# Order edges for the input and attention stages of a hybrid decoder block

## The chip, the cores and the metric

The kernel runs on one core of a Trainium2 chip. The metric is the device time of one launch in microseconds (us); three runs of the kernel before gave 2033.87, 2034.86 and 2029.52 us, median 2033.87. This kernel's runs of one program differ by up to 0.26%, so a difference within 0.3% (6 us) counts as no change here.

The core has five engines that each work through a queue of instructions in a fixed order: PE (matrix multiplication, with PEld for its weight loads), DVE (vector), ACT (scalar and evictions), POOL, and SP, which in this kernel issues nearly all DMAs. An instruction that waits for a semaphore holds up everything behind it on its own engine.

## The reference

One decoder layer on 1024 tokens plus 16 learned ones, model width 1024, in float32:

```python
xn = rms_norm(h, g_pre_mix)
b_c, c_c, h_c, q, k, v, g_conv, g_attn = split(xn @ w_in)      # 8 blocks of 1024
y_conv = b_c * causal_dwconv(c_c * h_c, conv_w_mix)
o = stick_breaking_attention(q, k, v)                          # 16 heads of 64
merged = sigmoid(g_conv + b0) * (y_conv @ w_proj_conv) \
       + sigmoid(g_attn + b1) * (o @ w_proj_attn)
h = h + rms_norm(merged @ w_out, g_post_mix)
u, g = split(rms_norm(h, g_pre_ffn) @ w_up_gate)               # 2 x 2816
h = h + rms_norm((gelu(causal_dwconv(u, conv_w_ffn)) * g) @ w_down, g_post_ffn)

# stick breaking, for z = q k / 8 and s < t:
A[t, s] = sigmoid(z_ts) * prod over s < j < t of (1 - sigmoid(z_tj));  o = A @ v
```

## The kernel before, in words

Every matrix product is made of three float32r matmuls on values split into a high and a low part: `hi` is a rounded copy (ACT, a CAST) and `lo` is what the rounding left (a subtraction on DVE or POOL). A weight block of 128x1024 is loaded by SP into a tile `raw`, becomes `whi` (line 457, ACT) and `wlo` (line 369, two halves on DVE or POOL), and then serves 24 steps of three matmuls each (lines 345 to 347).

The program has these stages in the trace: the input norm (to about 52 us); the input products with `w_in`, as plain blocks and as pairs by Strassen's method (52 to 558); attention (558 to 1014), in whose gaps PE computes 13 further blocks of gate columns of `w_in`; then the branch projections, `w_out`, the up projection and the down projection.

Attention goes by 8 pairs of heads, 2 heads per pair, and 3 groups of 3 query blocks (114 queries each) per head. For each head SP loads six tiles `qh`, `kk`, `ql` from DRAM (`load_h`, lines 934 to 941), and for each pair `vv` (`load_v`, lines 923 to 926). For a query block:

- PE makes the scores `z` (lines 965 and 966), ACT the sigmoids `fl` (line 971), and DVE one running product along the keys over `fl` in place (line 982, a TENSOR_TENSOR_SCAN of up to 1040 elements).
- Per block of keys, PE transposes the scanned `fl` into a PSUM tile `tp` (line 1001), ACT copies it to `ah` (line 1006), DVE subtracts to get `al` (line 447, the *lowering*), and PE multiplies `ah` and `al` with `vv` into `av` (lines 1016 and 1017).
- ACT and DVE or POOL add the finished `av` into `ot` (lines 1039 to 1046), which SP stores once per pair.

What sets the order: the input stage and the attention stage are each planned by the class `Plan`. It holds tasks with an engine, an estimated cost, a key and buffer slots, plays them through its own clock, and emits the instructions in the order in which that clock started them. The instructions then go to the framework's scheduler. It takes them with the emitted order as priority, but plays them through a cost model of its own, and where an instruction isn't ready by that model it may place a later one of the same engine ahead of it. What it arrives at is the fixed order of each engine's queue. The function `in_program_order` can forbid that for a range of instructions: it ties each instruction to the one before it on the same engine, by an edge that gives an order and no semaphore.

```python
def in_program_order(tc, nc, first, last):
    before = {}
    for ins in list(nc.cur_bb.bb.instructions)[first:last]:
        if ins.engine in before:
            tc.add_manual_dep(ins, before[ins.engine].name, ...)
        before[ins.engine] = ins
```

It is called once, in the last line of `block_kernel`, with `first` (the number of instructions when the input stage's plan begins, line 440) and `last` (the number when the attention stage's plan has run, line 1075). Much later, in the loop over the groups of the down projection, stands `last = gi == len(groups) - 1`. After that loop `last` is `True`, which in a slice is 1, so that in the kernel before the range is empty and no instruction is tied.

Of the kernel before, what the change touches and what calls it, by code (L numbers as in the profile page):

```python
# [135 lines left out]
def block_kernel(ctx, tc, x, meta_tokens, g_pre_mix, w_in, channels, w_proj_conv,  # L136
                 w_proj_attn, w_out, g_post_mix, g_pre_ffn, w_up_gate, w_down,
                 g_post_ffn, out):
    nc = tc.nc
# [297 lines left out]
    tmp_e = sring.tile([P, 512], F32, name="tmp_e")  # L437
    snap_t = sring.tile([P, 2, 3, HS], F32, name="snap_e")

    first = len(nc.cur_bb.bb.instructions)  # L440
    plan = Plan({"raw": 2, "whi": 0, "wlo": 0, "ap": 4, "wk": 5, "st": 8, "xw": 2})

    def engine_of(e):
# [287 lines left out]
    def strassen_pair(i, at):  # L731
# [49 lines left out]
        evacs = [[], []]  # L781
        made = [None, None]
        b = {}
        last = {}

        def product(k, s, which, start, tok, hold):
            name = names[k]
# [75 lines left out]
    for i in range(len(pairs1)):  # L863
        strassen_pair(i, at)
        at += 14 * prod
# [206 lines left out]
            plain(48 + 8 * which + ob, CH_Q, key, *outs,  # L1072
                  lambda: ps_mm.tile([P, 512], F32, name="mm", tag="mm"))
    plan.run()
    last = len(nc.cur_bb.bb.instructions)
    psA.close()

    work_ctx.close()
# [591 lines left out]
    for gi, fbs in enumerate(groups):  # L1670
        last = gi == len(groups) - 1
# [13 lines left out]
        for tb in range(8):  # L1685
# [23 lines left out]
            if last:  # L1709
# [3 lines left out]
                for hf in range(2):  # L1713
# [1 line left out]
                    nc.vector.scalar_tensor_tensor(a[:, c], a[:, c], r, hb[:, c],  # L1715
                                                   op0=ALU.mult, op1=ALU.add)
                    (nc.sync if hf else nc.scalar).dma_start(out[tb * P:(tb + 1) * P, c], a[:, c])
    in_program_order(tc, nc, first, last)


def in_program_order(tc, nc, first, last):
# [3 lines that stand above are left out]
            tc.add_manual_dep(ins, before[ins.engine].name,  # L1725
                              mybir.DependencyInfo(mybir.DependencyClass.NoSync,
                                                   mybir.DependencyReason.DATA),
                              reason="program order")
        before[ins.engine] = ins
# [57 lines left out]
```

## Time and profile before

| | |
|---|---|
| three runs | 2029.52, 2033.87, 2034.86 us |
| the profiled execution | 2030.09 us, of which 2028.3 us lie between its first and last instruction (the span) |
| PE busy | 1931.6 us, 95% of the span |
| DVE, ACT, POOL busy | 57%, 42%, 29% |
| granted TensorE clock, mean | 0.99 |

Each row of a timeline tells start and duration in us from the span's start, the engine (SPq is SP's queue of DMA issues), the line, the operation, the tile written and those read, and the count; square brackets hold the engine's idle time before it and what ended it. A window row has, for PE, PEld, DVE, ACT and POOL in this order, the busy time and in brackets the count of instructions, then the granted clock, the mean busy share of the 16 DMA engines and the GB/s they moved. The profile names tiles without their numbers; the listings of order below keep the numbers, which tell one buffer from the next.

### The profile page before, as it was taken

How to read it: one execution, taken by the hardware profiler on the slowest of the kernel's cores; microseconds unless marked ns; L12 is line 12 of the kernel's file. 1: busy time of each engine (PE TensorE's matmuls, PEld its weight loads, DVE VectorE, ACT ScalarE, POOL GpSimd, SP SyncE). 2: the span in 40 equal slices, each digit the busy share in tenths (PEclk: the TensorE clock that was granted, in tenths of full speed). 3: DMA queues.
4: the chain of work that ended last, by engine and by line, in shares of the span. 5: the costliest groups of instructions: out<-in, count | busy, mean ns of one | idle time of the engine just before them, and what ended most of it. 6: DMA issues, size and time to landing. Idle time of an engine off the chain costs nothing.

```text
span 2028.3 us, 32023 instructions
## 1 busy us (share of the span) xinstructions
PE 1931.6 (95%) x12732; PEld 1811.0 (89%) x12732; DVE 1161.1 (57%) x1784; ACT 842.6 (42%) x1766; POOL 580.1 (29%) x432
## 2 busy tenths in 40 slices
PE   6999999999988998989999999979999999999997
PEld 6999999999988888888899999968988998878886
DVE  6846666656368778787641116884354435345547
ACT  5533333444355566565541223453344344321122
POOL 1110000001101010010122560336555555654353
PEclk9999999999989999999999999989999999999999
DMA  3522222455684445441285673313221212253223
GB/s 137 161 84 74 83 64 64 145 143 166 181 187 127 118 128 128 113 117 58 84 271 148 188 211 124 105 32 118 70 84 63 104 63 84 75 182 117 84 84 135
DMA packets 73842, 238.56 MB, mean 118 GB/s; under 512 B 15400, under 2 KB 17224, under 8 KB 72668
## 3 DMA queue, kind: packets, MB, share of 16 engines
q1 hardware_dynamic: 70368, 226.00, 37.4%
q10 hardware_dynamic: 3324, 10.50, 1.6%
q8 instruction: 100, 1.64, 0.3%
q14 instruction: 50, 0.41, 0.1%
HBM read 166.02 MB, written 70.46 MB: 117 GB/s over the span
## 4 chain that ended last, share of the span: by engine, by line
PE 74%; DVE 13%; DMA 5%; ACT 3%; POOL 2%; issue 2%; SPq 0%; ACTq 0%; DVEq 0%; POOLq 0%
PE st L796 7%; PE st L799 7%; PE st L798 7%; PE st L1403 6%; PE st L1407 6%; PE st L1405 6%; DVE fl L982 5%; PE st L1697 3%; PE st L1695 3%; PE st L1696 3%; PE mm L245 2%; PE tp L1001 2%; PE mm L246 2%; PE mm L247 2%; DVE al L447 2%
## 5 line engine op out<-in xcount | busy, mean ns | idle before, releaser
L982 DVE TENSOR_TENSOR_SCAN fl<-fl,upper 114x128 f32<-114x128 f32 (+3 forms) x144 | 205.6, 1445 | 30.8 <-ACT fl L971 18.9
L173 POOL TENSOR_TENSOR a_op<-raw,a_op 128x512 fp32r<-128x512 f32 (+1 forms) x136 | 192.5, 1428 | 87.7 <-ACT a_op L172 85.5
L796 PE MATMUL st<-tT,s_op 128*128 128x260 f32 x672 | 190.9, 284 | 0.0
L799 PE MATMUL st<-tT,s_op 128*128 128x260 f32 x672 | 190.1, 283 | 0.0
L798 PE MATMUL st<-tT,s_op 128*128 128x260 f32 x672 | 190.0, 283 | 0.0
L1403 PE MATMUL st<-opT,a_op 128*128 128x258 f32 (+2 forms) x528 | 171.0, 324 | 5.2 <-ACT snap L1418 3.1
L1405 PE MATMUL st<-opT,a_op 128*128 128x258 f32 (+2 forms) x528 | 168.9, 320 | 2.6 <-DVE opT L173 1.7
L1407 PE MATMUL st<-opT,a_op 128*128 128x258 f32 (+2 forms) x528 | 168.7, 320 | 0.0
L1702 DVE TENSOR_TENSOR acc<-acc,st 128x512 f32<-128x512 f32 x144 | 98.4, 687 | 91.2 <-PE st L1697 91.2
L172 ACT CAST a_op<-raw 128x512 fp32r<-128x512 f32 (+1 forms) x136 | 85.1, 634 | 155.9 <-DMA raw<-in_w_up_gate_dram 52.7
L1006 ACT CAST ah<-tp 114x342 fp32r<-114x342 f32 (+3 forms) x288 | 105.8, 403 | 95.3 <-PE tp L1001 91.2
L447 DVE TENSOR_TENSOR al<-tp,ah 114x342 fp32r<-114x342 f32 (+3 forms) x288 | 118.0, 442 | 45.7 <-ACT ah L1006 44.1
L796 PE MATMUL st<-xnT,s_op 128*128 128x260 f32 x504 | 142.4, 283 | 0.0
L799 PE MATMUL st<-xnT,s_op 128*128 128x260 f32 x504 | 142.3, 282 | 0.0
L798 PE MATMUL st<-xnT,s_op 128*128 128x260 f32 x504 | 141.8, 281 | 0.0
L176 DVE TENSOR_TENSOR raw<-raw 128x512 f32<-128x512 f32 x72 | 73.8, 1026 | 108.1 <-POOL a_op L173 106.3
L751 ACT CAST s_op<-raw 128x512 fp32r<-128x512 f32 x126 | 78.2, 622 | 135.4 <-PE st L799 115.5
L447 DVE TENSOR_TENSOR s_op<-raw,s_op 128x512 fp32r<-128x512 f32 x121 | 84.4, 698 | 78.8 <-ACT s_op L751 78.3
L1017 PE MATMUL av<-al,vv 114*128 114x342 f32 (+3 forms) x288 | 92.1, 332 | 38.3 <-DVE al L447 37.5
L1405 PE MATMUL st<-opB,a_op 128*128 128x512 f32 (+2 forms) x396 | 127.4, 322 | 0.0
L1403 PE MATMUL st<-opB,a_op 128*128 128x512 f32 (+2 forms) x396 | 127.4, 322 | 0.0
L1407 PE MATMUL st<-opB,a_op 128*128 128x512 f32 (+2 forms) x396 | 126.9, 321 | 0.0
(224 smaller groups left out, 5880.4 us busy)
## 6 DMA issues: line engine op xcount, KB each, us to landing
raw<-in_w_in_dram SPq DMA_DIRECT2D x64, 512.0 KB
raw<-in_w_up_gate_dram SPq DMA_DIRECT2D x44, 512.0 KB
act_d<-owork SPq DMA_DIRECT2D x22, 512.0 KB
araw<-act_d SPq DMA_DIRECT2D x22, 512.0 KB
raw<-in_w_down_dram SPq DMA_DIRECT2D x22, 512.0 KB
qh<-qh_d SPq DMA_DIRECT2D x32, 256.5 KB
ql<-ql_d SPq DMA_DIRECT2D x32, 256.5 KB
vv_d<-vt SPq DMA_DIRECT2D x16, 512.0 KB
```

What stands on the lines that cost most here:

```text
L173: (lo_engine or nc.vector).tensor_tensor(lo, src, hi.bitcast(F32), op=ALU.subtract)
L447: eng.tensor_tensor(out, src, hi.bitcast(F32), op=ALU.subtract)
L796: nc.tensor.matmul(ps, wt[:, 0, c], xh, start=start and kb == 0, stop=False, skip_group_check=True)
L798: nc.tensor.matmul(ps, wt[:, 0, c], xl, start=False, stop=False, skip_group_check=True)
L799: nc.tensor.matmul(ps, wt[:, 1, c], xh, start=False, stop=kb == 3, skip_group_check=True)
L982: nc.vector.tensor_tensor_scan(fl[:, ::-1], fl[:, ::-1], upper[:, NT - nk:][:, ::-1], 1.0, op0=ALU.mult, op1=ALU.max)
L1006: nc.scalar.copy(kst["ah"][:n, off:], kst["tp"][:n, off:CH])
L1017: nc.tensor.matmul(av[:, off:], w, kst["al"][:n, off:], start=False, stop=(kb == nkb - 1))
L1403: nc.tensor.matmul(ps, wt[:, 0, k], xh, start=start and kb == 0, stop=False, skip_group_check=True)
L1405: nc.tensor.matmul(ps, wt[:, 0, k], xl, start=False, stop=False, skip_group_check=True)
L1407: nc.tensor.matmul(ps, wt[:, 1, k], xh, start=False, stop=stop and kb == 3, skip_group_check=True)
L1702: nc.vector.tensor_tensor(a, a, ps, op=ALU.add)
```

## The change

The two ends of the range get names that nothing else writes, so `in_program_order` ties the instructions of the input and the attention stage to the order in which the two plans emitted them, on PE, DVE, ACT, POOL and SP's queue. No instruction is added or removed, and no edge needs a semaphore. One line is removed ahead of line 784, so lines beyond it have numbers lower by one in the changed kernel (982 becomes 981, 939 becomes 938).

```diff
-    first = len(nc.cur_bb.bb.instructions)
+    pin_from = len(nc.cur_bb.bb.instructions)
     plan = Plan({"raw": 2, "whi": 0, "wlo": 0, "ap": 4, "wk": 5, "st": 8, "xw": 2})
...
         b = {}
-        last = {}
...
     plan.run()
-    last = len(nc.cur_bb.bb.instructions)
+    pin_to = len(nc.cur_bb.bb.instructions)
     psA.close()
...
-    in_program_order(tc, nc, first, last)
+    in_program_order(tc, nc, pin_from, pin_to)
```

The orders of the two kernels are alike over most of their length. On PE the first instruction that moves is a matmul at about 608 us of the trace, in the attention stage; 241 of PE's 12732 matmuls have another place, as have 297 of DVE's instructions, 157 of ACT's, 87 of SP's DMA issues and two of POOL's. Three places follow.

**SP's queue where the input stage ends.** `raw_6239` and `raw_6249` are the weights of the second and third gate block that attention interleaves; `ga_d<-gt_6048` stores the gate block that ends the input stage; the rows from line 939 on load the first head. Before:

```order
L358 DMA raw_6239<-in_w_in_dram 128x1024
L597 DMA vv_d_78<-vt_5868 128x1024
L597 DMA vv_d_78<-vt_5871 128x1024
L597 DMA vv_d_78<-vt_5887 114x256
L358 DMA raw_6249<-in_w_in_dram 128x1024
L552 DMA qh_d_74<-hi_5995 128x1026
L554 DMA ql_d_75<-su_5922 128x1026
L552 DMA kh_d_76<-hi_6021 128x1040
L554 DMA kl_d_77<-su_5953 128x1040
L939 DMA qh_6129<-qh_d_74 64x1026
L940 DMA kk_6131<-kh_d_76 64x1040
L941 DMA ql_6130<-ql_d_75 64x1026
```

In the changed kernel the same stretch has neither of the two weights, and the gate's store stands ahead of the first head's loads:

```order
L597 DMA vv_d_78<-vt_5887 114x256
L552 DMA qh_d_74<-hi_5995 128x1026
L554 DMA ql_d_75<-su_5922 128x1026
L552 DMA kh_d_76<-hi_6021 128x1040
L554 DMA kl_d_77<-su_5953 128x1040
L673 DMA ga_d_72<-gt_6048 128x1026
L938 DMA qh_6129<-qh_d_74 64x1026
L939 DMA kk_6131<-kh_d_76 64x1040
```

The two weights come after the loads of three heads and two pairs of `vv`:

```order
L939 DMA kk_6191<-kl_d_77 64x1040
L940 DMA ql_6190<-ql_d_75 64x1026
L924 DMA vv_6227<-vv_d_78 128x2048
L925 DMA vv_6227<-vv_d_78 114x256
L358 DMA raw_6239<-in_w_in_dram 128x1024
L358 DMA raw_6249<-in_w_in_dram 128x1024
L673 DMA ga_d_72<-gt_6175 128x1026
```

So `raw_6239` moved behind 30 other issues, `raw_6249` behind 27, and the store of `gt_6048` ahead of five loads that it followed.

**ACT at the start of attention.** `whi_6280` is the high part of `raw_6239`. Before, its cast stood ahead of the last eviction of the gate `gt_6048`:

```order
L670 ACTIVATE gt_6048<-st_6012,par_66 128x342
L670 ACTIVATE gt_6048<-st_6044,par_66 128x342
L457 CAST whi_6280<-raw_6239 128x1024
L670 ACTIVATE gt_6048<-st_6071,par_66 128x342
L670 ACTIVATE gt_6175<-mm_6125,par_66 128x342
```

In the changed kernel it stands 11 instructions later, behind the sigmoids of the first head's sixth query block:

```order
L970 ACTIVATE fl_6271<-z_6265 114x350
L970 ACTIVATE fl_6271<-z_6268 114x348
L457 CAST whi_6280<-raw_6239 128x1024
L670 ACTIVATE gt_6175<-mm_6245,par_66 128x342
L457 CAST whi_6294<-raw_6249 128x1024
L970 ACTIVATE fl_6309<-z_6287 114x406
```

What follows it, from `gt_6175<-mm_6245` on, now queues behind a cast that needs `raw_6239`. The two halves of `wlo_6281` made the same move on DVE, behind the scan of `fl_6271`.

**DVE in the middle of attention** (at 690 to 700 us of the trace). `fl` rows are scans, `al` rows lowerings. Before:

```order
L982 SCALAR_TENSOR_TENSOR fl_7724<-fl_7724,upper_6120 114x1040
L982 SCALAR_TENSOR_TENSOR fl_7751<-fl_7751,upper_6120 114x128
L1046 TENSOR_TENSOR ot_7769<-ot_7769,half_7770 64x342
L447 TENSOR_TENSOR al_7833<-tp_7765,ah_7784 114x342
L447 TENSOR_TENSOR al_7837<-tp_7772,ah_7789 114x342
L982 SCALAR_TENSOR_TENSOR fl_7796<-fl_7796,upper_6120 114x242
L982 SCALAR_TENSOR_TENSOR fl_7802<-fl_7802,upper_6120 114x356
L447 TENSOR_TENSOR al_7844<-tp_7778,ah_7808 114x228
L982 SCALAR_TENSOR_TENSOR fl_7813<-fl_7813,upper_6120 114x470
L982 SCALAR_TENSOR_TENSOR fl_7818<-fl_7818,upper_6120 114x584
L982 SCALAR_TENSOR_TENSOR fl_7835<-fl_7835,upper_6120 114x698
L447 TENSOR_TENSOR al_7873<-tp_7853,ah_7860 114x114
```

In the changed kernel:

```order
L981 SCALAR_TENSOR_TENSOR fl_7796<-fl_7796,upper_6120 114x242
L981 SCALAR_TENSOR_TENSOR fl_7802<-fl_7802,upper_6120 114x356
L447 TENSOR_TENSOR al_7873<-tp_7853,ah_7860 114x114
L447 TENSOR_TENSOR al_7879<-tp_7855,ah_7866 128x342
L447 TENSOR_TENSOR al_7883<-tp_7862,ah_7871 114x342
L981 SCALAR_TENSOR_TENSOR fl_7813<-fl_7813,upper_6120 114x470
L1045 TENSOR_TENSOR ot_7769<-ot_7769,half_7892 64x342
L447 TENSOR_TENSOR al_7914<-tp_7887,ah_7903 114x342
L447 TENSOR_TENSOR al_7920<-tp_7894,ah_7909 114x342
L981 SCALAR_TENSOR_TENSOR fl_7818<-fl_7818,upper_6120 114x584
L447 TENSOR_TENSOR al_7938<-tp_7899,ah_7918 114x342
L981 SCALAR_TENSOR_TENSOR fl_7835<-fl_7835,upper_6120 114x698
```

The scans of `fl_7813`, `fl_7818` and `fl_7835`, which stood in a row ahead of the lowering `al_7873`, now stand behind it and behind others. (The listing names the scan SCALAR_TENSOR_TENSOR; the profile calls it TENSOR_TENSOR_SCAN.)

## The prediction

> **What bounds the kernel now.** I read the page's busy shares first, then a table of windows by stage, then who waited for whom within attention.
>
> ```profile
> PE 1931.6 (95%) x12732; PEld 1811.0 (89%) x12732; DVE 1161.1 (57%) x1784; ACT 842.6 (42%) x1766; POOL 580.1 (29%) x432
> ```
> ```profile
> 52.00:558.00 506.00, 506.00 (x4074) 505.77 (x4072) 301.23 (x459) 205.34 (x412) 45.95 (x35) 1.00 0.39 117
> 558.00:1014.00 456.00, 409.07 (x2711) 381.54 (x2711) 345.88 (x493) 269.69 (x684) 50.86 (x36) 0.97 0.46 118
> 1014.00:1065.00 51.00, 47.74 (x302) 46.90 (x301) 22.95 (x49) 21.22 (x46) 11.60 (x16) 1.00 0.89 272
> ```
> ```profile
> PE av L1017 <- DVE al L447: 37.5, 32, 2.6
> ...
> PE tp L1001 <- DVE al L447: 2.9, 4, 0.7
> ```
>
> PE sets the time. In the input stage it is busy without a gap (506.00 of 506.00), so no order of the other engines can gain there, and one costs only if PE runs dry. In attention PE idles 456.0 - 409.1 = 46.9 us, and the last two rows (waits of PE from 572 to 1014 us: total, times, longest) put 40.4 us of it on the lowering `al`. This is all that a better order can win.
>
> Why is `al` late? Here are DVE and then PE around two of these stalls, and around a third.
>
> ```profile
> 627.70 3.23 DVE L982 TENSOR_TENSOR_SCAN fl<-fl,upper 114x926 f32<-114x926 f32 x1
> 630.85 0.67 DVE L447 TENSOR_TENSOR al<-tp,ah 114x114 fp32r<-114x114 f32 x2
> ...
> 695.56 3.89 DVE L982 TENSOR_TENSOR_SCAN fl<-fl,upper 114x470 f32<-114x470 f32 x3
> 699.37 1.08 DVE L447 TENSOR_TENSOR al<-tp,ah 114x114 fp32r<-114x114 f32 x3
> ...
> 681.64 2.84 DVE L982 TENSOR_TENSOR_SCAN fl<-fl,upper 114x812 f32<-114x812 f32 x1 [0.41 <-ACT fl L971]
> 684.41 0.97 DVE L447 TENSOR_TENSOR al<-tp,ah 114x114 fp32r<-114x114 f32 x3
> ```
> ```profile
> 631.15 0.32 PE L1017 MATMUL av<-al,vv 114*128 114x114 f32 x1 [2.58 <-DVE al L447]
> ...
> 699.67 0.32 PE L1017 MATMUL av<-al,vv 114*128 114x114 f32 x1 [1.91 <-DVE al L447]
> ...
> 684.71 0.32 PE L1017 MATMUL av<-al,vv 114*128 114x114 f32 x1 [1.16 <-DVE al L447]
> ```
>
> Each time a small lowering stands on DVE behind one or more scans. The scans can wait: the plan starts a group's transposes 0.6 of a head's time after its scores, 0.6 x 456 / 16 = 17 us as an estimate.
>
> **The change, first part: DVE in attention.** The plan's order has the lowering first at most of these places: the scan at 627.70 goes behind the lowering of 630.85, the three at 695.56 behind that of 699.37. The stall at 684.71 stays, for scan and lowering keep their places there; the same place comes three times (one for each stretch of two pairs of heads that follows the same pattern), 3 x 1.16 = 3.5 us. The tail of the last pair keeps about 1 us. So 40.4 - 4.5 = 36 us of stalls lose their cause. What a scan loses is the lowerings put ahead of it, 0.36 us each by the row of three (1.08 us), some 1 to 3 us against 17. DVE has room: 345.9 of 456 us busy. But DVE in a strict order will at times stand before a lowering whose `ah` isn't there, with scans ready behind it. Bounds: all 36, or half of it; I take 85%, 30 us, near the upper end, because the three stalls quoted have causes as long as themselves.
>
> After a long stall the clock falls as well. Five windows after stalls of 1.8 to 2.6 us show it (three other stalls of that length have none); first and last of the five:
>
> ```profile
> 584.20:587.60 3.40, 3.40 (x14) 3.25 (x13) 2.87 (x5) 2.28 (x6) 0.00 (x0) 0.50 1.02 313
> ...
> 959.60:963.00 3.40, 3.40 (x15) 3.33 (x16) 1.50 (x4) 2.53 (x6) 0.00 (x0) 0.51 0.00 0
> ```
>
> The granted clock is 0.50 for 3.4 us, which costs PE 1.7 us each, 8.5 in all; I take 7. The Trainium skill (TensorE: Matmul & The Clock Gate, Part 1: The HAM clock gate) has the clock fall after at least one idle window of about 3.4 us; by that, stalls of 2.6 us would cost no clock and the sum below would be 7 us worse, inside the range of the forecast A. The trace disagrees: its stalls are shorter than that, and 0.50 follows.
>
> **Second part: the front of attention.** Here the plan's order is worse. Before, SP issued `raw_6239` early, ACT cast it while PE finished the input stage, and PE used it as soon as it wanted:
>
> ```profile
> 528.53 0.33 SPq L358 DMA_DIRECT2D raw<-in_w_in_dram  x1
> ...
> 553.36 0.33 SPq L673 DMA_DIRECT2D ga_d<-gt  x1
> ```
> ```profile
> 551.85 1.05 ACT L457 CAST whi<-raw 128x1024 fp32r<-128x1024 f32 x1 [3.13 <-DMA kl_d<-su]
> ...
> 572.14 1.06 ACT L457 CAST whi<-raw 128x1024 fp32r<-128x1024 f32 x1 [0.76 <-issue]
> ...
> 573.53 0.90 ACT L971 ACTIVATE fl<-z 114x406 f32<-114x406 f32 x2
> ```
> ```profile
> 562.38 0.45 PE L966 MATMUL z<-kk,ql 128*114 128x128 f32 x1 [4.14 <-DMA ql<-ql_d]
> ...
> 573.32 0.41 PE L345 MATMUL mm<-xnT,whi 128*128 128x342 f32 x1
> ```
>
> In the changed kernel SP comes to `ga_d<-gt_6048`, waits until that gate is evicted (about 552.5, a cast of 1.05 us earlier than the 553.36 of before), and only then issues the first head's loads, the rest of three heads, two `vv`, and `raw_6239`. Their sizes, in the rows of DMA issues, and the rate at which the queue moved such data (last number, GB/s):
>
> ```profile
> raw<-in_w_in_dram SPq DMA_DIRECT2D x64, 512.0 KB
> qh<-qh_d SPq DMA_DIRECT2D x32, 256.5 KB
> ql<-ql_d SPq DMA_DIRECT2D x32, 256.5 KB
> vv<-vv_d SPq DMA_DIRECT2D x8, 1024.0 KB
> kk<-kh_d SPq DMA_DIRECT2D x16, 260.0 KB
> ga_d<-gt SPq DMA_DIRECT2D x8, 513.0 KB
> vv<-vv_d SPq DMA_DIRECT2D x8, 114.0 KB
> ```
> ```profile
> 545.00:550.00 5.00, 5.00 (x34) 5.00 (x33) 0.00 (x0) 0.55 (x1) 0.00 (x0) 1.00 0.84 127
> 550.00:555.00 5.00, 5.00 (x34) 5.00 (x33) 1.29 (x2) 1.49 (x2) 0.00 (x0) 1.00 1.05 267
> 552.50:591.00 38.50, 32.59 (x194) 31.18 (x193) 22.61 (x29) 17.59 (x44) 1.80 (x1) 0.87 1.04 225
> 590.00:595.00 5.00, 5.00 (x37) 4.79 (x35) 4.84 (x7) 3.06 (x8) 0.83 (x1) 1.00 1.00 199
> 738.00:742.30 4.30, 1.82 (x13) 1.46 (x11) 4.27 (x6) 1.40 (x4) 1.90 (x1) 1.00 0.85 348
> ```
>
> A head is 2 x 256.5 + 2 x 260 + 2 x 256.5 = 1546 KB. Gate 513, three heads 4638, two `vv` 2276 and the weight 512 make 7939 KB, 8.13 MB: 36.1 us at 225 GB/s. With some 2 us to start, `raw_6239` is there at 552.5 + 2 + 36.1 = 590.6 and `raw_6249` 2.3 us later, 592.9. ACT stands before `whi_6280` all this time, PE before the first matmul with it (573.32), DVE before its `wlo`; all sigmoids and `ah` of the first head queue behind. After the second cast (1.06) ACT takes up at 594.0 what it did at 573.53: 20.5 us later. The first scores lose little (562.38 becomes some 564) and lie within it. PE then starts at half clock, some 2 us. Loss 22 us. Bounds by the fastest and slowest rate of full queues above (267, 199): 15 to 29 us.
>
> The Trainium skill (DMA: Bandwidth & Descriptors, Anatomy of one DMA) counts about 2 us and bytes over 436 GB/s, fitted to single transfers of another issue path. By that, 8.13 MB take 20.7 us, the weight is there at 573.2, and the loss is some 4 us, an estimate from that page. The row with 1.04 busy engines and 225 GB/s decides for me.
>
> **Third part: edits at nothing.** In the input stage the largest move on SP puts a weight behind two stores:
>
> ```profile
> 92.39 0.34 SPq L358 DMA_DIRECT2D raw<-in_w_in_dram  x1
> ...
> 94.74 0.32 SPq L554 DMA_DIRECT2D ql_d<-su  x1
> ```
> ```profile
> 99.94 1.05 ACT L457 CAST whi<-raw 128x1024 fp32r<-128x1024 f32 x1 [3.18 <-PE st L346]
> ```
>
> That is 2.7 us of the 7.5 between the weight's issue and its cast, which waited for PE. If the rest is too short for the transfer, the cast comes about 1 us late, and PE's queue of plain blocks covers that. ACT's and DVE's swaps there hide behind PE's 506 us. Later weights that SP now issues after six head loads, and later casts (11 to 4 places back on ACT), are used tens of us later. After attention, moves are the scheduler's own consequences: PE idles 3.3 us there, so 0, within 3.
>
> **Sum.** -30 - 7 + 22 = -15 us. Against the profiled execution (2030.1, span 2028.3) that is 2015. The three runs shown have a mean of 2032.8 and a median 3.8 above the profiled execution, so for a median I say 2032.8 - 15 = 2018.
>
> **Rivals.**
>
> A, the forecast: 2018, itself 2009 to 2027 (loss 15 to 29 with most stalls gone). Chance 0.47.
>
> B, the front costs little: after the stores the queue runs at the 348 GB/s of the best window. Then 23.4 us bring the weight by 577.9, ACT takes up at 580.5, the loss is 7, and -30 us make 2003. For it speaks that 348 was seen; against, that it lasted 4 us, and that 38.5 us of nearly this mix gave 225. The page's rate would give 4 - 37 = -33, 2000. Chance 0.15.
>
> C, stalls move instead of going: PE, no longer held at one lowering, meets the next, whose transposes came from PE itself a moment before, and DVE idles for `ah`. Half of 36 and one fall of the clock remain as gain, 20 against 22: 2035. For it: DVE's lowerings waited 44 us for `ah` as it is (last numbers of the row). Against it: 24% of DVE's time in attention is idle. Chance 0.23.
>
> ```profile
> L447 DVE TENSOR_TENSOR al<-tp,ah 114x342 fp32r<-114x342 f32 (+3 forms) x288 | 118.0, 442 | 45.7 <-ACT ah L1006 44.1
> ```
>
>
> D, slower: the front decides. The queue moves 64-row tiles slowly; the window 545 to 550, just after SP had issued five such loads, shows 127 GB/s at 0.84 busy. At 140 the 8.65 MB up to the second weight take 61.8 us, ACT takes up at 617.4, the loss is 46, and +9 makes 2042. It decides from about 163 GB/s down, where 8.65 MB take 53 us and the loss is 37. Against it: 225 over 38.5 us of nearly the same mix. Chance 0.10.
>
> E, the edges change the listing and nothing that PE waits for: 2033. Against it stand the moved rows at the stalls quoted. Chance 0.05.
>
> **How the numbers follow.** Within 0.3% (6 us) counts as no change, about what runs of this kernel can tell. Faster: 0.42 of A, B, 0.06 of C, 0.63. Same: the rest of A, 0.15 of C, E, 0.25. Slower: D and 0.02 of C, 0.12. The range 2004 to 2036 takes in A and C and leaves out about half of B and all of D.
>
> **What would show it.** Right: in attention's wait rows `av` for `al` falls from 37.5 us to under 12; the scan of 926 stands behind the small lowering; five half-clock windows become one or two; and a single new stall of PE and ACT of 15 to 29 us appears near 573 us, ended by the cast of a weight that SP issued after the second `vv`. Wrong: no such stall (B), the waits for `al` still above 20 us (C), or DMA under 163 GB/s between 552 and 600 us (D).

## The result, and the profile after

The changed kernel took 2005.3 us (median of four runs, 2004.87 to 2008.8) where the kernel before took 2034.2 (median of four, 2029.52 to 2034.86) on the same chip: a ratio of 0.9867, with a 95% interval of 0.9848 to 0.9885. The profiled execution took 2004.87 us with a span of 2003.0, 25.3 us less than the span of before.

The page's busy shares after, the stages in windows, and PE's waits from 572 to 1014 us (total, times, longest):

```profile
PE 1923.8 (96%) x12732; PEld 1805.4 (90%) x12732; DVE 1155.4 (58%) x1784; ACT 840.8 (42%) x1766; POOL 583.9 (29%) x432
```
```profile
52.00:558.00 506.00, 504.81 (x4065) 504.49 (x4064) 297.88 (x456) 204.47 (x411) 45.44 (x35) 1.00 0.38 114
558.00:1014.00 456.00, 425.02 (x2848) 398.76 (x2849) 353.76 (x519) 280.97 (x713) 59.76 (x44) 0.97 0.51 136
```
```profile
PE mm L345 <- ACT whi L457: 14.3, 1, 14.3
PE av L1016 <- DVE al L447: 7.4, 12, 1.1
```

The 32 waits of `av` and 4 of `tp` for `al` (40.4 us) have become 12 waits of 7.4 us. One new wait of 14.3 us stands in their place. Two landmarks separate the two effects: PE's first matmul with the weight `raw_6239` (573.32 us before, quoted in the prediction), and its first matmul of the stage behind attention (line 245). This row is PE's timeline of the kernel before:

```profile
987.22 0.40 PE L245 MATMUL mm<-xnT,whi 128*128 128x342 f32 x1
```

And after:

```profile
588.80 0.65 PE L345 MATMUL mm<-xnT,whi 128*128 128x342 f32 x1 [14.31 <-ACT whi L457]
...
961.24 0.40 PE L245 MATMUL mm<-xnT,whi 128*128 128x342 f32 x1
```

The first landmark comes 15.5 us later, the second 26.0 us earlier. Between them lie 372.4 us instead of 413.9: **attention behind its front gained 41.5 us, the front lost 15.5**, and all that follows changed by 0.7 (-26.0 became -25.3 in the span). This is one pair of profiles; two more profiles of the kernel before, shown with the experiments, move the two terms by 2 to 5 us.

DVE and PE at the places that the prediction quotes. DVE after:

```profile
639.34 1.07 DVE L447 TENSOR_TENSOR al<-tp,ah 128x342 fp32r<-128x342 f32 x3
641.39 0.52 DVE L447 TENSOR_TENSOR al<-tp,ah 128x342 fp32r<-128x342 f32 x1 [0.99 <-ACT ah L1005]
641.83 2.08 DVE L981 TENSOR_TENSOR_SCAN fl<-fl,upper 114x926 f32<-114x926 f32 x1
...
686.43 1.85 DVE L981 TENSOR_TENSOR_SCAN fl<-fl,upper 114x812 f32<-114x812 f32 x1 [0.41 <-ACT fl L970]
688.20 0.97 DVE L447 TENSOR_TENSOR al<-tp,ah 114x114 fp32r<-114x114 f32 x3
...
700.43 1.08 DVE L447 TENSOR_TENSOR al<-tp,ah 114x114 fp32r<-114x114 f32 x3
701.44 1.12 DVE L981 TENSOR_TENSOR_SCAN fl<-fl,upper 114x470 f32<-114x470 f32 x1
```
```profile
640.78 0.28 PE L1016 MATMUL av<-al,vv 114*128 114x114 f32 x1
```

The scan of 926 columns (627.70 before) now stands behind the lowerings, the group of three lowerings (699.37 before) ahead of the scan of 470. PE's `av` at 640.78 waits for nothing; at the same matmul it had waited 2.58 us. The place at 684.41 of before has kept its order (686.43 and 688.20 here), and its stall of 1.16 us went all the same: the scan of 812 took 1.85 us instead of 2.84.

The front, on SP's queue and on ACT:

```profile
551.32 0.32 SPq L673 DMA_DIRECT2D ga_d<-gt  x1
...
576.09 1.58 SPq L358 DMA_DIRECT2D raw<-in_w_in_dram  x2
```
```profile
587.70 1.04 ACT L457 CAST whi<-raw 128x1024 fp32r<-128x1024 f32 x1 [15.42 <-DMA raw<-in_w_in_dram]
...
590.02 0.91 ACT L970 ACTIVATE fl<-z 114x406 f32<-114x406 f32 x2
```

SP comes to the two weights only at 576.09; the cast, which the profile says waited for this load, starts 11.6 us later. ACT takes up the sigmoid of 573.53 at 590.02, 16.5 us late.

### The profile page after: what moved, and what is told of

It is laid out like the page before. It is cut to its first block, busy times and chain, and to the rows that moved or that the text cites. A ratio compares the mean times of both kernels' runs of the same rounds, so it can differ in the third digit from the quotient of the medians.

```text
span 2003.0 us, 32017 instructions
## 1 busy us (share of the span) xinstructions
PE 1923.8 (96%) x12732; PEld 1805.4 (90%) x12732; DVE 1155.4 (58%) x1784; ACT 840.8 (42%) x1766; POOL 583.9 (29%) x432
## 4 chain that ended last, share of the span: by engine, by line
PE 78%; DVE 10%; DMA 4%; ACT 3%; issue 2%; POOL 2%; SPq 0%; ACTq 0%; DVEq 0%; POOLq 0%
PE st L795 7%; PE st L798 7%; PE st L797 7%; PE st L1402 6%; PE st L1406 6%; PE st L1404 6%; PE st L1696 3%; PE st L1694 3%; PE st L1695 3%; DVE fl L981 3%; PE mm L246 3%; PE mm L245 3%; PE mm L247 3%; PE tp L1000 2%; PE av L1016 2%
## 5 line engine op out<-in xcount | busy, mean ns | idle before, releaser
L981 DVE TENSOR_TENSOR_SCAN fl<-fl,upper 114x128 f32<-114x128 f32 (+2 forms) x144 | 202.2, 1419 | 33.4 <-ACT fl L970 32.2
L798 PEld LDWEIGHTS st<-tT,s_op 128*128 128x128 f32 x672 | 126.9, 189 | 0.0
L797 PEld LDWEIGHTS st<-tT,s_op 128*128 128x128 f32 x672 | 126.5, 188 | 0.0
```

Of the source, the lines that this page charges most:

```text
L797: nc.tensor.matmul(ps, wt[:, 0, c], xl, start=False, stop=False, skip_group_check=True)
L798: nc.tensor.matmul(ps, wt[:, 1, c], xh, start=False, stop=kb == 3, skip_group_check=True)
L981: nc.vector.tensor_tensor_scan(fl[:, ::-1], fl[:, ::-1], upper[:, NT - nk:][:, ::-1], 1.0, op0=ALU.mult, op1=ALU.max)
```

## The experiments

The theory T: the change is two separable things. DVE's order in attention gains some 43 us by matched matmuls of the two traces, and SP's order at the front, which brings `raw_6239` late, loses some 16. The rivals were that the gain needs all engines tied together, that the late weight costs less than its stall, that the stalls came from a DVE that was late as a whole and not from single scans, and that the queue itself is the limit at the front.

The two groups of runs were on chips where the kernel before took 2031.06 us (the first four runs) and 2025.24 (the next four); ratios hold within a group. The times in the expectations are worked out from the first chip, where the two kernels took 2034 and 2005 us, so that the landmarks decide more than the times do. Behind the second landmark the twelve profiles took 1034.4 to 1041.8 us, a spread of 7 us that no run here explains; the kernel before and the changed one are the two longest there.

| run | median, us | ratio to before, 95% interval | first landmark | second | between |
|---|---|---|---|---|---|
| before | | 1 | 573.3 | 987.2 | 413.9 |
| before, second profile | | | 570.9 | 989.6 | 418.7 |
| before, third profile | | | 570.3 | 988.0 | 417.7 |
| the change | 2005.3 | 0.9867 (0.9848 to 0.9885) | 588.8 | 961.2 | 372.4 |
| DVE alone tied | 1981.9 | 0.9757 (0.9734 to 0.9780) | 570.5 | 942.8 | 372.3 |
| all but DVE tied | 2054.9 | 1.0127 (1.0101 to 1.0153) | 589.1 | 1013.2 | 424.1 |
| weights free | 1985.9 | 0.9781 (0.9759 to 0.9802) | 576.0 | 947.8 | 371.8 |
| attention alone tied | 1998.2 | 0.9843 (0.9822 to 0.9864) | 587.8 | 960.4 | 372.6 |
| weights after head 1 | 1986.2 | 0.9798 (0.9776 to 0.9820) | 573.9 | 945.8 | 371.9 |
| weights after head 2 | 1994.5 | 0.9839 (0.9817 to 0.9862) | 578.4 | 954.0 | 375.6 |
| scan first at four places | 2017.8 | 0.9962 (0.9943 to 0.9982) | 589.9 | 979.2 | 389.3 |
| attention alone, weights free | 1977.3 | 0.9760 (0.9732 to 0.9787) | 567.5 | 939.4 | 371.9 |

**DVE alone tied**, in `in_program_order`:

```diff
     for ins in list(nc.cur_bb.bb.instructions)[first:last]:
+        if ins.engine != nc.vector.engine:
+            continue
```

> Only DVE's instructions of the range are tied to the plan's order; PE, ACT, POOL and SP are left to the scheduler as before the change, so that the weight raw_6239 is issued early again. Theory T (the change is two things: DVE's order in attention gains some 43 us, the late weight on SP costs some 16): 2005 - 15 = 1990 (1984 to 1996), no stall of PE over 6 us near 573 us, waits of av for al under 12 us. Rival R1 (the gain needs PE, ACT and DVE tied together, since a DVE in strict order meets engines in another order): 2012 to 2032, with waits for al above 20 us. Rival R2 (the late weight costs less than the stall shows, since PE makes the time up later): 2002 to 2006.

Measured: 1981.9 us, better than T's range. PE's waits for `al` and the second landmark of this run:

```profile
PE av L1016 <- DVE al L447: 8.4, 9, 1.2
```
```profile
942.80 0.41 PE L245 MATMUL mm<-xnT,whi 128*128 128x342 f32 x1
```

The edges on one queue bring the whole gain of attention (372.3 us between the landmarks, as with all five engines tied), and without SP's and ACT's edges there is no loss at the front. R1 and R2 fall. The scheduler, given these edges, also chose another order than before on PE (82 matmuls at least have another place), ACT and SP, so it is the run with the scan first, below, that moves DVE's order and nothing else.

**All but DVE tied**, the reverse:

```diff
     for ins in list(nc.cur_bb.bb.instructions)[first:last]:
+        if ins.engine == nc.vector.engine:
+            continue
```

> All engines of the range are tied except DVE, whose order the scheduler chooses again. Theory T: the gain of attention goes and the late weight stays: 2034 + 16 = 2050 (2042 to 2056), waits of av for al at 35 us or more, and the stall near 573 us still there. Rival R1 (PE's, ACT's and SP's order carry part of the gain): 2010 to 2030. Rival R2 (the late weight costs little in the sum): 2032 to 2038.

Measured: 2054.9 us, 26 us slower than before by the ratio, the loss without the gain.

```profile
PE av L1016 <- DVE al L447: 37.0, 32, 2.6
PE mm L345 <- ACT whi L457: 14.3, 1, 14.3
PE tp L1000 <- DVE al L447: 3.1, 3, 1.0
```

The front's wait is that of the changed kernel, the waits for `al` are those of before (40.1 us against 40.4). R1 and R2 fall here too. Yet the time between the landmarks is 10.2 us longer than before. That was not in the expectation; the last two runs below are for it.

**Weights free.** The loads of `raw_6239` and `raw_6249` are left out of SP's chain; PE, ACT, DVE and POOL keep the order of the changed kernel to the last instruction.

```diff
-                st["raw"] = load_raw(o)
+                st["raw"] = load_raw(o); free is None or free.append(nc.cur_bb.bb.instructions[-1])
...
     for ins in list(nc.cur_bb.bb.instructions)[first:last]:
+        if ins.name in free:
+            continue
```

> The changed kernel with one difference: the loads raw_6239 and raw_6249 (the weights of attention's second and third gate block) have no place in SP's tied order; the scheduler puts them ahead of the last stores of the input stage. Every other instruction on every engine stands as in the changed kernel. Theory T: the new stall near 573 us goes and nothing else changes, 2005 - 15 = 1990 (1986 to 1994). Rival R3 (the queue is the limit: with the weights first, the heads arrive later and PE waits for these instead): 1999 to 2006, with a longer first wait of z for ql. Rival R4 (ACT's cast stands late in its order anyway): 1997 to 2005.

Measured: 1985.9 us, at the lower edge of T's range. The first matmul with the weight waits for nothing:

```profile
576.00 0.40 PE L345 MATMUL mm<-xnT,whi 128*128 128x342 f32 x1
```

The place of two issues on SP is worth 12.8 us at this landmark (588.80 to 576.00) and nothing behind it (371.8 us against 372.4). By the ratios it is 0.0086, 17.5 us; of the 17.9 us between the two spans 4.5 lie behind the second landmark, so the landmarks are the safer number. R3 and R4 fall, though the 5.3 us that the first scores wait for `kk` stay, as R3 says of a part.

**Attention alone tied.** The range begins where attention's plan is made:

```diff
-    FL = [2] * 6 + [1] * 3
+    FL = [2] * 6 + [1] * 3; pin_from = len(nc.cur_bb.bb.instructions)
```

> Only the instructions of the attention stage are tied, those of the input stage are left to the scheduler; the five loads of the first head then stand ahead of the last gate's store on SP, and raw_6239 stays behind three heads and two vv. Theory T: the input stage is bound by PE in either order, the gain in attention stays whole, and the weight comes earlier by the 5 to 7 us that SP no longer waits for the gate: 1999 (1994 to 2003), stall of PE near 573 us 6 to 11 us. Rival R5 (tying the input stage has a part in the gain): 2008 to 2025. Rival R6 (the queue was full in any case, so that an earlier issue brings nothing): 2004 to 2007, stall still 14 to 16 us.

Measured: 1998.2 us, T's number, but not for T's reason. The stall is longer, not shorter:

```profile
587.78 0.66 PE L345 MATMUL mm<-xnT,whi 128*128 128x342 f32 x1 [16.43 <-ACT whi L457]
```

The first scores come 4.0 us earlier (558.09 instead of 562.08), and PE then waits longer for a weight that comes 1.0 us earlier. That is what R6 says of the front, though not its 2004 to 2007. At the second landmark this kernel is 0.9 us ahead of the changed one; the rest of the 4.8 us between the spans lies behind attention, 2.8 of it in one wait at 1174 us that the profile of this run doesn't have. R5 falls: tying the input stage has no part in the gain (372.6 us between the landmarks without it, 372.4 with it).

**Weights after the first head, and after the second.** The two loads get a fixed place in SP's chain, 16 or 8 issues ahead of the one that the plan gave them, and nothing else moves:

```diff
+    at = names.index(moved[0].name) - 16
+    sp = sp[:at] + moved + [i for i in sp[at:] if i.name not in [m.name for m in moved]]
...
-    for ins in list(nc.cur_bb.bb.instructions)[first:last]:
+    for ins in rows:
```

> The changed kernel with the loads raw_6239 and raw_6249 tied to another place on SP: behind the gate's store and the first head, ahead of vv and the second and third head. Nothing else moves on any engine. Theory T' (the weight comes when the bytes ahead of it have passed at some 225 GB/s): 513 + 1546 + 512 KB are 2.63 MB, 11.7 us, landing near 566, before PE wants it at some 573; no stall of PE by the cast of whi, 2005 - 14 = 1991 (1987 to 1997). Rival R6' (the weights, 4.7 us of the queue, delay vv and the second head so that PE waits there instead): a stall of 3 to 5 us on z or av, 1995 to 2000.

> As the run before, with the two loads behind the gate's store, the first head, vv and the second head (14 issues), ahead of the third head. Theory T': 513 + 1546 + 1138 + 1546 + 512 KB are 5.38 MB, 23.9 us at 225 GB/s, landing near 578.4; a stall of PE by the cast of whi of 5 to 8 us, 1996 (1992 to 2001), between the changed kernel and the one with the loads after the first head. Rival R7 (the loss isn't in proportion to the bytes ahead, the queue's depth holds the issue): 2003 to 2007, stall of 12 to 15 us.

Measured: 1986.2 and 1994.5 us. After the first head no wait of PE for the cast is left, and behind the first scores no wait of `z` or `av` is over 1.2 us, so that R6' falls. After the second head there are two new stalls:

```profile
565.82 2.11 SPq L358 DMA_DIRECT2D raw<-in_w_in_dram  x2
```
```profile
578.39 0.43 PE L345 MATMUL mm<-xnT,whi 128*128 128x342 f32 x1 [3.45 <-ACT whi L457]
582.54 0.73 PE L964 MATMUL z<-kk,qh 128*114 128x464 f32 x1 [2.17 <-ACT fl L970]
```

The cast started at 577.29, where 2 us to start and 23.9 us of bytes from 552.5 had put the landing at 578.4. The second stall is that of a sigmoid behind the cast of the second weight, for which ACT had waited too. So the first landmark follows the bytes ahead of the weight: 573.9 us after one head, 578.4 after two, 588.8 after three and both `vv`. The stall by the cast, 3.5 us, is shorter than the 5 to 8 that T' said; with the second one it is 5.6. R7 falls.

**Scan first.** At four places, one for each two pairs of heads, the scan of 926 columns goes ahead of the two lowerings that the plan puts before it:

```diff
+        if dve[k].name in scans7 and (lows.get(dve[k - 2].name), lows.get(dve[k - 1].name)) == (114, 342):
+            dve[k - 2:k + 1] = [dve[k], dve[k - 2], dve[k - 1]]
```

> The changed kernel with DVE's tied order altered at four places, once in each stretch of two pairs of heads: the scan of 926 columns stands ahead of the two lowerings (114 and 342 columns) that the plan puts before it, as the scheduler had it. Theory T (each such place is a stall of PE of 2.0 to 2.6 us, and where PE is busy for less than half of one of the clock's 3.41 us windows, a window at half clock for 1.7 us more): 4 x 2.4 + about half of 4 x 1.7 = 13, 2018 (2013 to 2024), waits of av for al at 16 to 18 us instead of 7.4. Rival R8 (a tied order has slack enough for one scan, the stalls came from DVE being late as a whole): 2004 to 2008, waits for al up to 10 us.

Measured: 2017.8 us. DVE, PE, PE's waits and two windows at the first of the places:

```profile
641.57 3.22 DVE L981 TENSOR_TENSOR_SCAN fl<-fl,upper 114x926 f32<-114x926 f32 x1
644.72 0.67 DVE L447 TENSOR_TENSOR al<-tp,ah 114x114 fp32r<-114x114 f32 x2
```
```profile
645.01 0.32 PE L1016 MATMUL av<-al,vv 114*128 114x114 f32 x1 [2.57 <-DVE al L447]
```
```profile
PE av L1016 <- DVE al L447: 17.5, 16, 2.6
```
```profile
642.10:645.50 3.40, 0.83 (x9) 0.70 (x8) 3.28 (x3) 0.57 (x2) 0.75 (x1) 1.00 0.75 305
645.50:648.90 3.40, 3.40 (x15) 3.32 (x14) 0.93 (x2) 2.27 (x6) 0.00 (x0) 0.50 0.00 0
```

Four moved scans cost 16.9 us between the landmarks, 4.2 each: 2.5 of stall (7.4 to 17.5 us in four more waits) and 1.7 that come with a window at half clock behind each of the four. R8 falls: one scan ahead of the lowerings makes the stall. PE's, ACT's, POOL's and SP's orders are those of the changed kernel. Of each 2.5 us some 1.1 come from the scan itself, which took 3.16 to 3.22 us at these places, where POOL was at work as it began, and 2.08 in the changed kernel (the last section comes back to this).

**Attention alone, weights free**, the two edits together:

> Only the attention stage is tied, and within it the loads raw_6239 and raw_6249 are free (the two edits of the runs before together). Theory T: the stall by the late weight goes, and with the first head's loads ahead of the gate's store the first scores wait 3 us less: 1986 - 3 = 1983 (1979 to 1988). Rival R9 (the queue is the limit, the first scores wait as long as in the changed kernel): 1985 to 1989.

Measured: 1977.3 us; the first landmark is at 567.50, earlier than in any other run:

```profile
567.50 0.41 PE L345 MATMUL mm<-xnT,whi 128*128 128x342 f32 x1
```

PE's first wait for the first head's loads is 2.0 us, where the changed kernel has 5.3 and 0.8, so that R9 falls. With a ratio of 0.9760 it is as fast as DVE alone tied (0.9757). Both beat the kernel before and the changed one.

**The kernel before, profiled twice more.** It is to settle why equal stalls cost 10 us more in the run with all but DVE tied.

> The kernel before, unchanged, profiled once more. Theory G (the granted clock is set once in each 3.41 us of a grid that lies otherwise in each execution; a grid window in which PE is busy for less than about half is followed by one at 0.50): the waits of av and tp for al are again 40 us (39 to 42) at the same places, but the half-clock windows between 590 and 1010 us are other ones and of another number than the four of the first profile, 0 to 10, each worth 1.7 us of span; every one of them follows a grid window in which PE was busy for less than 0.6. Rival H (the stalls themselves decide, by their length or the work around them): the same four windows, after the same stalls.

> The kernel before, unchanged, profiled a third time, for a third place of the grid. Theory G: as for the run before; spans of the profiles differ by 1.7 us for each half-clock window of 3.4 us more or less (within 2 us). Rival H: the same four windows after the same stalls as in the first profile.

The first of the two has a span of 2025.0 us, the other 2027.9. The same stall of 2.51 us near 740 us shows it best. First the kernel before in its first profile, then in the second, in windows of 3.4 us on the grid of the clock's own changes:

```profile
737.80:741.20 3.40, 2.02 (x14) 1.66 (x12) 3.37 (x4) 1.60 (x5) 1.90 (x1) 1.00 0.78 312
741.20:744.60 3.40, 2.27 (x17) 2.25 (x18) 2.43 (x5) 1.89 (x6) 0.00 (x0) 1.00 0.37 149
```
```profile
734.60:738.00 3.40, 1.47 (x11) 1.10 (x9) 3.40 (x3) 1.04 (x4) 1.81 (x1) 1.00 0.86 355
738.00:741.40 3.40, 2.83 (x12) 2.76 (x13) 1.87 (x5) 2.08 (x6) 0.00 (x0) 0.50 0.19 77
```

In the first profile an edge of the grid cuts the stall in two, PE is busy for 2.02 and 2.27 us of the two windows, and the clock stays. In the second 1.9 us of the stall lie in one window, PE is busy for 1.47 us of it, and the clock falls. In all three profiles every change of the clock lies on a grid of 3.413 us, which begins elsewhere in each. Between 590 and 1010 us the half clock took four windows in the first profile, eight in the second and eight in the third, with waits of `av` for `al` of 37.5, 36.4 and 36.5 us. Of the windows at full clock in which PE was busy for less than half (14 in the three profiles), all were followed by one at 0.50; of those at 0.51 to 0.60, three of ten; above that none. Three windows that were themselves at 0.50 were followed by another, though PE was busy for 0.78 to 0.84 of them. Rival H falls.

What a window costs is best read from PE's busy time between the landmarks, for the same matmuls. First the three profiles of the kernel before, then the run with all but DVE tied, then the changed kernel:

```profile
573.32:987.22 413.90, 371.96 (x2485) 346.28 (x2484) 324.53 (x459) 250.80 (x642) 47.72 (x32) 0.98 0.45 115
570.92:989.57 418.65, 377.67 (x2485) 351.84 (x2484) 324.94 (x459) 252.13 (x642) 47.56 (x32) 0.96 0.44 115
570.33:988.03 417.70, 376.71 (x2486) 350.89 (x2484) 325.39 (x459) 252.23 (x643) 47.56 (x32) 0.97 0.44 115
```
```profile
589.14:1013.23 424.09, 381.52 (x2483) 357.32 (x2483) 329.14 (x461) 252.66 (x643) 54.74 (x32) 0.95 0.40 107
```
```profile
588.80:961.24 372.44, 363.28 (x2483) 340.01 (x2483) 319.98 (x462) 249.95 (x643) 50.77 (x32) 1.00 0.46 122
```

Between the landmarks the half clock lasted 5.0, 9.0 and 8.3 windows in the three profiles, and PE was busy 5.7 and 4.8 us longer in the second and third than in the first while it idled 1.0 us less: 1.4 us for each window more, where 1.7 was expected. The run with all but DVE tied had 12.1 such windows there, 7.1 more than the first profile; 9.6 of its 10.2 us are busy time, again 1.4 for each, and 0.6 idle time.

The expectation for the whole spans missed. With 1.7 us for each window more they should have grown; they were 2025.0 and 2027.9 against 2028.3. The second profile reached the first landmark 2.4 us earlier and took 5.7 us less behind the second one; in the third it was 3.0 and 1.2 us.

## Why the prediction was right, and where not

The time of 2005.3 us lies in the range of 2004 to 2036, but only 1.3 us above its lower end, 12.7 us under the 2018 that was forecast and below the 2009 to 2027 that A itself gave. That the number fell inside is in part luck. The mechanism was that of A, and the signs named for it came: `av` for `al` fell to 7.4 us, the scan of 926 stands behind the lowering, and one new stall near 573 us is ended by the cast of a weight that SP issued behind the second `vv`. It was 14.3 us long on PE and 15.4 on ACT, at the lower end of the 15 to 29 that had been named. Of the five half-clock windows none is left between the landmarks; one new one stands at the stage's end, and the new stall has its own. Two sizes were off, and both errors go the same way.

- **Stalls that lose their cause: 36, of which 30 taken.** The waits fell by 33.0 us (40.4 to 7.4), between the two. The bound of half was far off: a tied DVE did not wait more for `ah`, it waited less:

```profile
L447 DVE TENSOR_TENSOR al<-tp,ah 114x342 fp32r<-114x342 f32 (+3 forms) x288 | 115.8, 441 | 28.0 <-ACT ah L1005 27.0
```

  That is 28.0 us of idle time from 588 to 1004 us, where the row of before had 45.7; rival C rested on that row. A PE that is not held back can deliver its transposes earlier, which would explain it; no run separates that. The 3.5 us that were to stay at the unmoved place went, and small waits of up to 1.1 us elsewhere stayed instead. The edges on DVE did not remove them. With DVE alone tied all three are there (1.16 us each; DVE and PE at the first):

```profile
667.57 2.84 DVE L981 TENSOR_TENSOR_SCAN fl<-fl,upper 114x812 f32<-114x812 f32 x1 [0.41 <-ACT fl L970]
```
```profile
670.63 0.32 PE L1016 MATMUL av<-al,vv 114*128 114x114 f32 x1 [1.16 <-DVE al L447]
```

- **The clock: 8.5, of which 7 taken.** With 33.0 us of stalls, 8.5 of the 41.5 are left, which looks like the five windows at 1.7. But the new stall keeps 0.9 of a window, so 4.1 are gone, and the repeated profiles put one at 1.4: this is some 6 of clock and 2 to 3 of something not separated. The price was also not the kernel's own: another execution of the kernel before has eight such windows where this one had four.
- **The front: 22 taken, 15 to 29 as bounds; measured 15.5.** This is the term that failed most. The queue was faster than the 225 GB/s of the mixed window, as the row of this stretch shows:

```profile
552.50:587.60 35.10, 15.93 (x87) 15.10 (x85) 6.11 (x6) 4.31 (x10) 0.00 (x0) 0.77 0.99 242
```

  At 242 GB/s the same 8.13 MB take 33.6 us, and the gate's store was 1.2 us earlier, so that the cast began at 587.70 and not at 590.6. The other two profiles of the kernel before reach the first landmark at 570.9 and 570.3, so that against these the front lost 17.9 and 18.5 us; 22 was too much against all three. The second weight came right behind the first, so that ACT lost 16.5 us instead of 20.5. The two more that were set for the start at half clock were there:

```profile
578.40:592.10 13.70, 3.30 (x10) 2.86 (x11) 3.12 (x4) 4.23 (x9) 1.79 (x1) 0.50 0.76 219
```

  PE runs its first 3.3 us behind the stall at 0.50, which lies between the landmarks and not in the 15.5. But the kernel before had a stall and a half-clock window of its own at 584 us, which this one swallowed; the prediction counted that among the gains, so it is part of the 41.5.
- **Edits at nothing.** Right: the input stage ends no later (its last gate's store issues at 551.32, 553.36 before), and with it tied or not attention takes the same time behind the first landmark (372.4 and 372.6 us).
- **The sum.** -30 - 7 + 22 = -15 was the forecast; 15.5 - 41.5 + 0.7 = -25.3 is what the profiles show. By the other two profiles of the kernel before it is 17.9 - 46.2 + 6.3 = -22.0 and 18.5 - 45.3 + 1.9 = -24.9. The rest of the way to 28.9 us between the medians is that the profile of before was one of its faster executions, 2030.09 us against the median of 2034.2.

B is not what happened, though its time of 2003 is nearer than A's: the front cost 15.5, not 7, and the gain was larger. D's 163 GB/s was not come near.

The prediction said that the trace disagrees with the Trainium skill (TensorE: Matmul & The Clock Gate, Part 1: The HAM clock gate), since stalls shorter than 3.4 us were followed by half clock. That was read too narrowly. The same section says that the window of 3413 ns runs free of the kernel, and the grid in the three profiles of the kernel before is just that. What the runs add is that a window need not be idle: less than half busy was enough (14 of 14 windows).

## To carry to other kernels

Where a plan's order is to be forced on a scheduler, force it on the queue whose order was seen to be wrong in the trace, and look at every other queue's order before tying it: here DVE's edges gained all and SP's lost over a third of it, by two loads behind 30 others. The later these loads stood on the full queue in the runs above, the later they landed, so a load that one engine wants at a known time belongs in front of prefetches for later. A stall of two to three us on PE should be priced with the chance of a clock window behind it, not with a fixed surcharge, and two kernels that differ by less than 0.5% should be compared over several executions.

## What the chip showed beside that

- **The clock's grid.** Nine executions of the kernel before on one chip had spans from 2018.7 us (mean granted clock 0.990) to 2031.4 us (0.983). The grid's place can be one reason for such a spread: nearly the same waits gave four half-clock windows between 590 and 1010 us or eight. It is not the only one, for the two profiles with eight had the shorter spans.
- **A scan that begins while GpSimd is at work is longer.** The scan of 926 columns took 2.08 us in the changed kernel and 3.22 in the run that put it first, where POOL was at work as it began (from 640.95 to 642.85 us); the scan of 812 took 2.84 us before and 1.85 after. In the profile before, POOL was running when this scan began; after, it began 1.0 us behind the scan's start, and its two pieces took 4.93 us instead of 2.53:

```profile
680.25 2.53 POOL L369 TENSOR_TENSOR wlo<-raw,whi 128x512 fp32r<-128x512 f32 x2 [20.38 <-ACT whi L457]
```
```profile
687.47 4.93 POOL L369 TENSOR_TENSOR wlo<-raw,whi 128x512 fp32r<-128x512 f32 x2 [22.85 <-PE z L965]
```

  The Trainium skill (SBUF — State Buffer, section SBUF: two separate sides) says that a DVE instruction with two inputs in SBUF and a GpSimd instruction that reads SBUF take a shared pair of ports in turn, each for the whole instruction. The trace agrees as far as these durations go: whichever began second took longer. So the stall at 684.71 went with POOL's timing and not with the edges on DVE; with DVE alone tied, the scan at 667.57 begins beside a POOL instruction and takes 2.84 us again.
- **SP's lead.** On a full queue SP issued some 11.5 us ahead of the cast that waited for the load: 576.09 to 587.70 in the changed kernel, 565.82 to 577.29 with the weights after the second head. The rest of the wait passes on SP itself, where the profile shows no wait of a load but a late issue.
